# Middle two column groups of an output projection by seven block products instead of eight, and matmuls on zeros at the start

## The chip, the core and the metric

One NeuronCore of a Trainium2 chip runs the whole layer. The metric is device time in microseconds from launch to end, as the median of three runs. TensorE is called PE here, its weight loads PEld, VectorE is DVE, ScalarE is ACT, GpSimd is POOL and SyncE is SP. PE, DVE, ACT and POOL each work through their own queue strictly in the order in which the program was laid down, and an instruction starts when the semaphores that it names have been raised. SP only starts transfers.

## The reference

The layer takes 512 tokens of 2048 channels (and 16 learned tokens ahead of them as further keys), normalises them, multiplies by one wide input projection, runs two attention mixers of 8 heads each, gates both with SiLU, and joins the heads to a matrix of 512 x 2048. What follows is the part that the change is about:

```python
y = jnp.einsum('blc,cd->bld', jnp.concatenate([ya, yb], axis=-1), w_out[layer])
h = h + rmsnorm(y, post_norm_g[layer])
```

The output projection is thus a product of 512 x 2048 by 2048 x 2048, and after it each token's 2048 results are scaled by one number that needs the squares of all of them.

## The kernel before

Everything is float32 in and out. For TensorE each operand is split in two parts of a reduced format, a high part (made by ACT, which rounds) and a low part (made by DVE, the remainder), and each product is three matmuls: high by high, low by high, high by low. The function `wload` (line 142) does it for weights: SP loads 128 x 1024 weights into `st`, ACT writes `wh` (line 150), DVE writes `wl` (line 151). There are three buffers of each, so that the split of a chunk waits until PE has finished with the chunk three before it.

A work list `todo` holds the weight chunks of the whole layer in order of use, and `fetch` hands them out and starts loads two chunks ahead. While PE works through the input projection, tasks (`Lanes`) are put between its matmuls for the attention of the heads; PE's order is the order in which the Python code calls it, while the other engines' instructions are placed by a scheduler with priorities. The negative number `AHEAD` sets how urgent the weights' splits are.

The output projection (`dense_out`, line 723) makes the 2048 output columns in four groups of 512. A group needs 8 chunks of weights, each of which holds 2 of the 16 blocks of 128 rows; for each block and each of the 4 token blocks there are three matmuls of 128 x 128 by 128 x 512, so that a chunk feeds 24 matmuls and a group 192. The stationary operand is the joined heads, `oh` and `ol`, split once and held for all groups: the heads of mixer B and half of mixer A go through a DRAM scratch `oscr` first, the last four heads come straight from SBUF. Group 0 is mixed with the end of the attention. When a group is done, `collect` (line 767) sums squares on ACT and multiplies by the gain `gpB` on DVE, for each of 4 tiles `y` of 128 tokens. In the last group `finish` (line 773) is called for one token block after the other; it makes the scale on POOL, and adds the input `xr` on DVE, except for the last 512 columns, where ACT and POOL do it; SP stores the pieces.

At the start, the first 8 chunks of x and of weights are loaded together (line 207): for each of 16 blocks of x, ACT and DVE make `xh` and `xl`, and 12 matmuls follow.

Of the kernel before, what the change touches and what calls it, by code (L numbers as in the profile page):

```python
# [17 lines left out]
P = 128  # L18
# [90 lines left out]
def kernel(ctx: ExitStack, tc: tile.TileContext, xT, xn, xm, w_s, w_t, w_q, w_o,  # L109
# [19 lines left out]
    oscr = [dr.tile([2, P, SEQ], F32, name=f"oscr{i}", tag=f"oscr{i}") for i in range(6)]  # L129

    def ctile(shape, name, dt=F32, src=None):
        t = cst.tile(shape, dt, name=name, tag=name)
        if src is not None:
            load(t, src)
        return t
# [6 lines left out]
    def wload(src, n=1024, dma=nc.sync.dma_start, parts=1):  # L142
        st = wp.tile([P, 1024], F32, name="st", tag="st")
        wh = wp.tile([P, 1024], F32R, name="wh", tag="wh")
        wl = wp.tile([P, 1024], F32R, name="wl", tag="wl")
        for i in range(parts):
            c = slice(i * n // parts, (i + 1) * n // parts)
            dma(out=st[:, c], in_=src if parts == 1 else src[:, c])
            with tc.high_priority(AHEAD):
                nc.scalar.activation(wh[:, c], st[:, c], AF.Copy)  # L150
                nc.vector.tensor_tensor(out=wl[:, c], in0=st[:, c], in1=wh[:, c].bitcast(F32),  # L151
                                        op=ALU.subtract)
        return wh, wl

# [3 lines left out]
    nc.scalar.activation(warm, epst, AF.Identity)  # L158
    gcol = ctile([P, KT], "gcol")
# [22 lines left out]
    def fetch(ahead=2):  # L182
        while todo and len(chunks) <= ahead:
            chunks.append(wload(todo.pop(0)))
# [81 lines left out]
    cosT = ctile([P, TT, P], "cosT", src=cos_d)  # L266
    sinT = ctile([P, TT, P], "sinT", src=sin_d)
    gqB = ctile([P, P], "gqB", src=gq)
    gkB = ctile([P, P], "gkB", src=gk)
# [235 lines left out]
    def attention_A(h, qn, q_task, k, k_task, v, v_task):  # L505
# [43 lines left out]
        over[NH + h] = last  # L549
        if h < 4:  # L550
            over[NH + h] = lanes.spawn(spill_A(h), 0.0, last)
# [112 lines left out]
    for grp in range(4):  # L664
        todo += [w_o[grp, :, k0:k0 + 2, :] for k0 in range(0, KT, 2)]
# [90 lines left out]
    yp = ctx.enter_context(tc.tile_pool(name="yp", bufs=1))  # L756
    pd2 = ctx.enter_context(tc.tile_pool(name="pd2", bufs=4, space=PSUM))
# [3 lines left out]
    xr = [yp.tile([P, DM], F32, name=f"xr{t}", tag=f"xr{t}") for t in range(TT)]  # L761
    ssy = [yp.tile([P, 4], F32, name=f"ssy{t}", tag=f"ssy{t}") for t in range(TT)]
    for t in range(TT):
        nc.sync.dma_start(out=xr[t], in_=xn[t * P:(t + 1) * P, :])
    sspart = [yp.tile([P, 1], F32, name=f"ssp{t}", tag=f"ssp{t}") for t in range(TT)]

    def collect(g, t, ps):
        gs = slice(g * 512, (g + 1) * 512)
        jk = yp.tile([P, 512], F32, name="jko", tag="jko", bufs=2)
        nc.scalar.activation(jk, ps, AF.Square, accum_out=ssy[t][:, g:g + 1])  # L770
        nc.vector.tensor_tensor(out=y[t][:, gs], in0=ps, in1=gpB[:, gs], op=ALU.mult)

    def finish(t, ps):
# [6 lines left out]
        cuts = [0, 256, 896, 1536, 2048] if last else [0, 1024, 2048]  # L780
        for i, (c0, c1) in enumerate(zip(cuts, cuts[1:])):
            cs = slice(c0, c1)
            if last and i == 3:
                nc.scalar.activation(y[t][:, cs], y[t][:, cs], AF.Copy, scale=r)
                nc.gpsimd.tensor_tensor(out=y[t][:, cs], in0=y[t][:, cs], in1=xr[t][:, cs],
                                        op=ALU.add)
            else:
                nc.vector.scalar_tensor_tensor(out=y[t][:, cs], in0=y[t][:, cs], scalar=r,
                                               in1=xr[t][:, cs], op0=ALU.mult, op1=ALU.add)
            load(out[t * P:(t + 1) * P, cs], y[t][:, cs])  # L790

    for g in range(3):
        pss = first if g == 0 else dense_out(g, pd2 if g % 2 else pd)
        for t in range(TT):
# [65 lines left out]
```

## Time and profile before

| | us |
|---|---|
| median of three runs | 958.59 (957.73 to 961.38) |
| the profiled execution | 958.46 |
| its span, first to last instruction | 956.5 |
| PE busy | 934.7 |
| DVE busy | 525.5 |
| ACT busy | 457.9 |
| POOL busy | 127.7 |
| moved by DMA | 99.31 MB |

The span is 2.0 us shorter than the execution's own time; what lies around it is taken to be the same for both kernels. A row of a timeline gives start, duration, engine, line, operation, the tile written and the tiles read, and a count where equal ones are merged; in brackets stands how long the engine was idle before and who released it. A row of the grouped view gives the busy time and the mean of one in nanoseconds, and then the idle time ahead of them. Matmuls are pipelined: the time that one takes of PE is the distance between two starts, not its duration.

### The profile page before, as it was taken

What the parts mean: (1) busy time and instruction counts of PE and PEld (TensorE: products, weight loads), DVE (VectorE), ACT (ScalarE), POOL (GpSimd) and SP (SyncE); (2) the same over time, 40 slices, a digit from 0 to 9 for tenths busy, and PEclk for the clock granted to TensorE, in tenths of its full rate; (3) what the DMA queues carried; (4) which work ended last, traced back from release to release, by engine and by line L of the source; (5) the groups of instructions that cost most, each with busy time, mean ns of one, the idle gap of its engine ahead of it and who ended that gap; (6) DMA issues with size and microseconds to landing.
All of it is one profiled execution on the core that took longest, in us unless ns stands there. A gap on an engine that the chain in (4) does not pass through costs nothing.

```text
span 956.5 us, 13979 instructions
## 1 busy us (share of the span) xinstructions
PE 934.7 (98%) x5530; PEld 818.2 (86%) x5530; DVE 525.5 (55%) x900; ACT 457.9 (48%) x812; POOL 127.7 (13%) x211
## 2 busy tenths in 40 slices
PE   7999999999999999999999999998999999999996
PEld 6889898989989898998998888886888888888884
DVE  6276675747575574756654274447554663232325
ACT  6665555547464553746552253354555742221221
POOL 0001010101001010100201041225212120000002
PEclk9999999999999999999999999998999999999999
DMA  9752222322223122222223223111222344623314
GB/s 318 252 180 77 85 90 68 97 77 94 82 73 104 66 99 77 86 82 68 91 75 94 94 66 110 57 66 56 77 77 67 114 128 158 238 88 98 101 45 175
DMA packets 31426, 99.31 MB, mean 104 GB/s; under 512 B 3681, under 2 KB 5601, under 8 KB 30721
## 3 DMA queue, kind: packets, MB, share of 16 engines
q1 hardware_dynamic: 31216, 98.42, 31.1%
q8 instruction: 43, 0.70, 0.3%
q14 instruction: 23, 0.18, 0.1%
q10 hardware_dynamic: 144, 0.01, 0.0%
HBM read 91.07 MB, written 7.34 MB: 103 GB/s over the span
## 4 chain that ended last, share of the span: by engine, by line
PE 89%; DVE 4%; ACT 2%; DMA 2%; POOL 2%; issue 1%; SPq 0%; DVEq 0%; POOLq 0%; ACTq 0%
PE pd L63 55%; PE po L63 19%; PE sc L63 6%; PE pv L63 5%; PE tr L66 5%; DMA xns<-in_xn_dram 2%; DVE qn L567 1%; DVE wl L151 1%; POOL ssh L228 1%; ACT qn L639 0%; ACT jk L564 0%; PE ss L63 0%; POOL qn L581 0%; ACT p L537 0%; DMA gcol<-in_gpre_dram 0%
## 5 line engine op out<-in xcount | busy, mean ns | idle before, releaser
L63 PE MATMUL pd<-xh,wh 128*128 128x264 f32 (+1 forms) x992 | 334.8, 337 | 4.9 <-ACT wh L150 4.9
L63 PE MATMUL pd<-xh,wl 128*128 128x264 f32 (+1 forms) x992 | 326.4, 329 | 0.3 <-DVE wl L151 0.3
L63 PE MATMUL pd<-xl,wh 128*128 128x264 f32 (+1 forms) x992 | 326.1, 329 | 0.0
L150 ACT ACTIVATE wh<-st 128x1024 fp32r<-128x1024 f32 (+2 forms) x139 | 144.4, 1039 | 278.0 <-PE po L63 95.8
L151 DVE TENSOR_TENSOR wl<-st,wh 128x1024 fp32r<-128x1024 f32 (+2 forms) x139 | 167.2, 1203 | 176.0 <-ACT wh L150 174.7
L63 PEld LDWEIGHTS pd<-xh,wh 128*128 128x128 f32 x992 | 188.4, 190 | 17.6 <-ACT wh L150 4.9
L63 PEld LDWEIGHTS pd<-xh,wl 128*128 128x128 f32 x992 | 187.7, 189 | 18.0 <-DVE wl L151 0.7
L63 PEld LDWEIGHTS pd<-xl,wh 128*128 128x128 f32 x992 | 188.6, 190 | 11.6
L63 PE MATMUL po<-wh,ol 128*128 128x512 f32 x256 | 101.0, 395 | 0.9 <-DVE ol L296 0.9
L63 PE MATMUL po<-wl,oh 128*128 128x512 f32 x256 | 101.9, 398 | 0.0
L63 PE MATMUL po<-wh,oh 128*128 128x512 f32 x256 | 101.7, 397 | 0.0
L450 ACT ACTIVATE p<-p,mx 128x528 f32<-128x528 f32 x64 | 46.5, 728 | 34.2 <-POOL mx L447 34.0
L63 PEld LDWEIGHTS po<-wh,ol 128*128 128x128 f32 x256 | 48.1, 188 | 12.2 <-DVE ol L296 1.2
L440 DVE CUSTOM_DVE_ANT_0 p<-sc,dist 128x528 f32<-128x528 f32 x64 | 44.9, 701 | 24.0 <-PE sc L63 23.5
L63 PEld LDWEIGHTS po<-wl,oh 128*128 128x128 f32 x256 | 48.1, 188 | 11.2
L63 PEld LDWEIGHTS po<-wh,oh 128*128 128x128 f32 x256 | 48.1, 188 | 10.2
L63 PE MATMUL pd<-wh,xh 128*128 128x512 f32 x128 | 52.2, 408 | 0.8 <-DVE vf L287 0.8
L293 ACT ACTIVATE ph<-tr 128x512 fp32r<-128x512 f32 x64 | 37.6, 591 | 31.2 <-PE tr L66 30.9
L296 DVE TENSOR_TENSOR pl<-tr,ph 128x512 fp32r<-128x512 f32 x64 | 43.4, 688 | 16.1 <-ACT ph L293 14.9
L66 PE MATMUL tr<-ident,p 128*128 128x128 f32 (+1 forms) x320 | 50.8, 273 | 0.8 <-DVE pl L296 0.8
L63 PE MATMUL pd<-wh,xl 128*128 128x512 f32 x128 | 50.6, 395 | 0.0
L63 PE MATMUL pd<-wl,xh 128*128 128x512 f32 x128 | 50.5, 395 | 0.0
(161 smaller groups left out, 1292.1 us busy)
## 6 DMA issues: line engine op xcount, KB each, us to landing
st<-in_w_t_dram SPq DMA_DIRECT2D x82, 512.0 KB, 3.6
st<-in_w_o_dram SPq DMA_DIRECT2D x32, 512.0 KB, 3.6
st<-in_w_q_dram SPq DMA_DIRECT2D x16, 512.0 KB, 3.6
xs<-in_xT_dram SPq DMA_DIRECT2D x16, 264.0 KB, 5.1
xns<-in_xn_dram SPq DMA_DIRECT2D x8, 512.0 KB, 6.3
xr<-in_xn_dram SPq DMA_DIRECT2D x4, 1024.0 KB, 10.2
os<-oscr SPq DMA_DIRECT2D x6, 512.0 KB, 3.6
out_dram<-y SPq DMA_DIRECT2D x6, 512.0 KB, 2.7
```

Of the source, the lines that this page charges most:

```text
L63: self._add(self.nc.tensor.matmul(out, lhsT, rhs, start=start, stop=stop), us)
L66: self._add(self.nc.tensor.transpose(out, in_, ident), 0.109)
L150: nc.scalar.activation(wh[:, c], st[:, c], AF.Copy)
L151: nc.vector.tensor_tensor(out=wl[:, c], in0=st[:, c], in1=wh[:, c].bitcast(F32), op=ALU.subtract)
L228: nc.gpsimd.tensor_tensor(out=dst, in0=dst, in1=mhalf[:rows, :dst.shape[1]], op=ALU.pow)
L293: nc.scalar.activation(dst, src, AF.Copy)
L296: nc.vector.tensor_tensor(out=dst, in0=src, in1=h.bitcast(F32), op=ALU.subtract)
L440: nc.vector.tensor_tensor_reduce(out=two(p), in0=sc[:, :, :HALF], in1=two(dist[:, w0:w0 + NT]), scale=1.0, scalar=-3.0e38, op0=ALU.add, op ...
L450: nc.scalar.activation(p2[m], p2[m], AF.Exp, scale=0.125, bias=mx[:, m:m + 1], accum_out=sm[:, m:m + 1])
L567: nc.vector.scalar_tensor_tensor(out=raw[:, i, :], in0=raw[:, i, :], scalar=ss[:rows, i:i + 1], in1=g[:rows], op0=ALU.mult, op1=ALU.mult)
```

## The change

**The seven products.** Groups 0 and 3 stay as they are. Groups 1 and 2 are seen as a product of 2 x 2 blocks: two halves of the tokens, two halves of the 2048 summed channels (first the heads of mixer B, then those of mixer A), two column groups. Plainly these are eight block products. In their place stand seven, in the way of Strassen and Winograd: four of them multiply sums of blocks. Each block product takes 4 chunks of weights and 2 token blocks, 12 matmuls to a chunk, 48 in all.

- Weights: tiles `ch0` to `ch3` hold a running sum of blocks. POOL's queue loads block (1, 0) and then adds (1, 1) by an accumulating transfer; after each split (`wsplit`, ACT and DVE as before) the next block is loaded into `st` and added on DVE (`summed`).
- Heads: the halves of `oscr` (now all 16 heads are written there) are loaded into a ring of five tiles `ts`, on POOL's queue for the first two sums (`first_sums`) and on SP's for the others. DVE forms the sums, ACT and DVE split them (`operand`).
- Results: products leave PSUM by an ACT copy or by DVE sums into the tiles `y`; the squares are taken by ACT from `y`, and the gain is multiplied on POOL (`block_done`).
- The input `xr` is loaded on POOL's queue, in 16 pieces, into tiles that the operands leave; `finish` adds in pieces of 512 columns.
- The priority of the weight splits is changed (`rank`) once the attention is over.

**The zeros.** A tile `heat` of 128 x 256 zeros is written by DVE, and 16 matmuls multiply it by itself ahead of all others.

```diff
+    heat = ctile([P, 256], "heat", F32R, pool=ap)
+    nc.vector.memset(heat.bitcast(F32), 0.0)
+    hot = pd.tile([P, 512], F32, name="hot", tag="pd")
+    for i in range(16):
+        mm(hot[:, :256], heat[:, :P], heat, start=True, stop=True)
...
+    def summed(add=None, fresh=None):
+
+        def step(i):
+            ws = wsplit(chain[i])
+            if fresh:
+                nc.sync.dma_start(out=chain[i], in_=block(*fresh, i))
+            if add:
+                st = wp.tile([P, 1024], F32, name="st", tag="st")
+                nc.sync.dma_start(out=st, in_=block(*add, i))
+                with tc.high_priority(rank[0]):
+                    nc.vector.tensor_tensor(out=chain[i], in0=chain[i], in1=st, op=ALU.add)
+            return ws
+        return [lambda i=i: step(i) for i in range(4)]
...
+    todo += whole(0) + plain(0, 0) + plain(0, 1) + summed((0, 0)) + summed((0, 1))
+    todo += summed((1, 0), fresh=(0, 0)) + summed() + plain(1, 1) + whole(3)
...
+    rank[0] = 40
...
+    def heads_of(i, half, dma):
+
+        t = yp.tile([P, 2, NP], F32, name="ts", tag="ts", bufs=5)
+        dma.dma_start(out=t, in_=oscr[i].rearrange("i p q -> p i q")[:, :, half])
+        return t
+
+    def operand(tag, i, src):
+
+        h, l = [yp.tile([P, 2, NP], F32R, name=f"{tag}{x}{i}", tag=f"{tag}{x}{i}") for x in "hl"]
+        hi(h, src)
+        lo(l, src, h)
+        return h, l
+
+    for i in range(4):
+        chain[i] = yp.tile([P, 1024], F32, name=f"ch{i}", tag=f"ch{i}")
+        nc.gpsimd.dma_start(out=chain[i], in_=block(1, 0, i))
+    t1, t2, t3, t4 = [], [], [], []
+
+    def first_sums(i):
+        b0, b1, a1 = [heads_of(j, half, nc.gpsimd)
+                      for j, half in ((i, lo_), (i, hi_), (4 + i, hi_))]
+        nc.gpsimd.dma_start(out=chain[i], in_=block(1, 1, i), accum_op=ALU.add)
+        TTv(out=b0, in0=b1, in1=b0, op=SUB)
+        t1.append(operand("u", i, b0))
+        TTv(out=a1, in0=a1, in1=b0, op=SUB)
+        t2.append(operand("v", i, a1))
+
+    def third_sum(i):
+        b1, a1 = heads_of(i, hi_, nc.sync), heads_of(4 + i, hi_, nc.sync)
+        TTv(out=a1, in0=a1, in1=b1, op=SUB)
+        t3.append(operand("u", i, a1))
+
+    def fourth_sum(i):
+        a0 = heads_of(4 + i, lo_, nc.sync)
+        TTv(out=a0, in0=t2[i][0].bitcast(F32), in1=a0, op=SUB)
+        TTv(out=a0, in0=a0, in1=t2[i][1].bitcast(F32), op=ALU.add)
+        t4.append(operand("v", i, a0))
...
+    def product(ops, pool):
+
+        pss = [pool.tile([P, 512], F32, name="po", tag="pd") for _ in range(2)]
+        for i in range(4):
+            wh, wl = fetch()
+            for u in range(2):
+                for j in range(2):
+                    bh, bl = ops(i, j, u)
+                    c = slice(j * 512, (j + 1) * 512)
+                    mm(pss[u], bh, wh[:, c], start=(i + j == 0), stop=False)
+                    mm(pss[u], bl, wh[:, c], start=False, stop=False)
+                    mm(pss[u], bh, wl[:, c], start=False, stop=(i + j == 4))
+        return pss
...
+    def block_done(r, x, u):
+        g = 1 + r
+        square(2 * x + u, g, C(r, x, u))
+        TTp(out=C(r, x, u), in0=C(r, x, u), in1=gpB[:, g * 512:(g + 1) * 512], op=ALU.mult)
...
+    for i in range(4):
+        first_sums(i)
+    for u, ps in enumerate(product(of_y(0, 0), pd2)):
+        nc.scalar.activation(C(1, 0, u), ps, AF.Copy)
+    for u, ps in enumerate(product(of_y(1, 0), pd2)):
+        TTv(out=C(0, 0, u), in0=ps, in1=C(1, 0, u), op=ALU.add)
+        block_done(0, 0, u)
+    for u, ps in enumerate(product(of_t(t1), pd)):
+        nc.scalar.activation(C(1, 1, u), ps, AF.Copy)
+    for i in range(4):
+        third_sum(i)
+    for u, ps in enumerate(product(of_t(t2), pd)):
+        TTv(out=C(1, 0, u), in0=ps, in1=C(1, 0, u), op=SUB)
+        TTv(out=C(0, 1, u), in0=C(1, 0, u), in1=C(1, 1, u), op=ALU.add)
+    for i in range(4):
+        fourth_sum(i)
+    for u, ps in enumerate(product(of_y(1, 1), pd2)):
+        TTv(out=C(0, 1, u), in0=ps, in1=C(0, 1, u), op=SUB)
+        block_done(0, 1, u)
+    for u, ps in enumerate(product(of_t(t3), pd2)):
+        TTv(out=C(1, 0, u), in0=C(1, 0, u), in1=ps, op=SUB)
+        TTv(out=C(1, 1, u), in0=C(1, 0, u), in1=C(1, 1, u), op=ALU.add)
+        block_done(1, 1, u)
+    for u, ps in enumerate(product(of_t(t4), pd)):
+        TTv(out=C(1, 0, u), in0=C(1, 0, u), in1=ps, op=SUB)
+        block_done(1, 0, u)
...
```

In what follows the seven products are called P1 to P7 in this order, and their 28 chunks of weights c0 to c27.

**DVE, groups 1 and 2.** In the kernel before, DVE's whole work for a group of 45 us is eight splits and four products by the gain (the rows are those of group 1):

```order
L771 TENSOR_TENSOR y_8191<-po,gpB 128x512
L771 TENSOR_TENSOR y_8192<-po,gpB 128x512
L771 TENSOR_TENSOR y_8193<-po,gpB 128x512
L151 TENSOR_TENSOR wl<-st,wh 128x1024
L771 TENSOR_TENSOR y_8194<-po,gpB 128x512
L151 TENSOR_TENSOR wl<-st,wh 128x1024 x7
```

In the changed kernel this is DVE's queue from the split of c20 (the first row, for the start of P6) to that of c21 (the last); `ts` and `vl` belong to the operands of P7, `ch_8220` to chunk c23:

```order
L155 TENSOR_TENSOR wl<-ch_8214,wh 128x1024
L701 TENSOR_TENSOR ch_8220<-ch_8220,st 128x1024
L309 TENSOR_TENSOR vl_8681<-ts,vh_8680 128x512
L842 TENSOR_TENSOR ts<-ts,vl_8279 128x512
L841 TENSOR_TENSOR ts<-vh_8295,ts 128x512
L841 TENSOR_TENSOR ts<-vh_8312,ts 128x512
L842 TENSOR_TENSOR ts<-ts,vl_8296 128x512
L309 TENSOR_TENSOR vl_8689<-ts,vh_8688 128x512
L842 TENSOR_TENSOR ts<-ts,vl_8313 128x512
L309 TENSOR_TENSOR vl_8697<-ts,vh_8696 128x512
L155 TENSOR_TENSOR wl<-ch_8216,wh 128x1024
```

Between two splits that followed each other directly there now stand one sum of weights and eight operations on operands of the next product. Over the stretch from the first operand's sum (line 829) to the split of c21, DVE's queue holds 30 operations of 128 x 1024 (18 splits and 12 sums of weights) and 41 of 128 x 512.

**POOL's queue.** Before, POOL had nothing to do from the end of the attention to the first `ry`. Now, after the last row of the attention (`pm`), it starts these transfers:

```order
L413 TENSOR_SCALAR pm<-pm 32x256 x3
L822 DMA ch_8214<-in_w_o_dram 128x1024
L822 DMA ch_8216<-in_w_o_dram 128x1024
L822 DMA ch_8218<-in_w_o_dram 128x1024
L822 DMA ch_8220<-in_w_o_dram 128x1024
L810 DMA ts<-oscr_78 128x2x256 x2
L810 DMA ts<-oscr_82 128x2x256
L828 DMA ch_8214<-in_w_o_dram 128x1024
L810 DMA ts<-oscr_79 128x2x256 x2
L810 DMA ts<-oscr_83 128x2x256
L828 DMA ch_8216<-in_w_o_dram 128x1024
L828 DMA ch_8218<-in_w_o_dram 128x1024
```

The same queue goes on with the rest of the first operands, and then with its first two products by the gain:

```order
L810 DMA ts<-oscr_80 128x2x256 x2
L810 DMA ts<-oscr_84 128x2x256
L810 DMA ts<-oscr_81 128x2x256
L828 DMA ch_8220<-in_w_o_dram 128x1024
L810 DMA ts<-oscr_81 128x2x256
L810 DMA ts<-oscr_85 128x2x256
L889 TENSOR_TENSOR y_8224<-y_8224,gpB 128x512
L889 TENSOR_TENSOR y_8225<-y_8225,gpB 128x512
```

The rows of line 828 are the accumulating transfers. The loads of the third and fourth operand pair (`oscr_80`, `oscr_81`) stand behind them, and each `ts` also waits until DVE has done with the tile of the ring that it takes.

116 lines of the change are left out of this document (71 added, 45 removed).

## The prediction

> **What bounds the kernel now.** I read the busy times first, then what PE waits for, then the timeline of the output projection.
>
> ```profile
> PE 934.7 (98%) x5530; PEld 818.2 (86%) x5530; DVE 525.5 (55%) x900; ACT 457.9 (48%) x812; POOL 127.7 (13%) x211
> PE pd L63 <- ACT wh L150: 4.9, 1, 4.9
> PE sc L63 <- ACT p L537: 3.0, 1, 3.0
> PE tr L63 <- DVE rm L247: 1.3, 1, 1.3
> ```
>
> The second to fourth rows are what PE waited for in all, how often and the longest. Ahead of the first matmul it waits 4.9 us, and nowhere else over 3 us: PE sets the time, and what is to be seen is whether it keeps doing so where the change puts work on others. The timeline of ACT shows the groups' length, and windows over groups 1 and 2 show what the others do there:
>
> ```profile
> 811.27 0.60 ACT L770 ACTIVATE jko<-po 128x512 f32<-128x512 f32 x1 [2.68 <-PE po L63]
> ...
> 856.02 0.60 ACT L770 ACTIVATE jko<-po 128x512 f32<-128x512 f32 x1 [2.68 <-PE po L63]
> ...
> 900.82 0.60 ACT L770 ACTIVATE jko<-po 128x512 f32<-128x512 f32 x1 [2.68 <-PE po L63]
> core 0: us, PE busy (x) PEld busy (x) DVE busy (x) ACT busy (x) POOL busy (x), PEclk, DMA share, GB/s
> 813.00:858.00 45.00, 45.00 (x195) 36.19 (x194) 12.68 (x13) 11.21 (x18) 0.00 (x0) 1.00 0.49 174
> 858.00:903.00 45.00, 45.00 (x195) 36.19 (x194) 12.62 (x14) 11.21 (x19) 0.00 (x0) 1.00 0.31 94
> ```
>
> The first squares of two groups start 44.8 us apart (900.82 - 856.02). That is 192 matmuls at 233 ns, without a gap, while DVE works 12.7 us of 45 and POOL none. DVE has over 30 us of room in each group, which the change uses up.
>
> **The change part by part.** (1) *Removed matmuls.* 56 blocks of 12 for 64: 336 matmuls for 384, so 48 x 0.233 = 11.2 us less, all on the path. A product lasts 11.2 us now, and a chunk is used up in 2.8 us where it lasted 5.6.
>
> (2) *The zeros.*
>
> ```profile
> 4.89 0.59 PE L63 MATMUL pd<-xh,wh 128*128 128x264 f32 x1 [4.89 <-ACT wh L150]
> ...
> 6.97 1.62 ACT L167 ACTIVATE xh<-xs,gcol 128x528 fp32r<-128x528 f32 x2
> 7.23 0.63 PE L63 MATMUL pd<-xl,wh 128*128 128x512 f32 x1
> ...
> 7.65 0.63 PE L63 MATMUL pd<-xh,wl 128*128 128x512 f32 x1
> 7.74 1.65 DVE L168 SCALAR_TENSOR_TENSOR xl<-xs,gcol,xh 128x528 fp32r<-128x528 f32 x2 [0.32 <-ACT xh L167]
> ...
> 11.02 0.40 PE L63 MATMUL pd<-xl,wh 128*128 128x512 f32 x1
> 11.25 0.39 PE L63 MATMUL pd<-xh,wl 128*128 128x512 f32 x1
> ...
> 12.18 0.28 PE L63 MATMUL pd<-xh,wh 128*128 128x264 f32 x1
> ```
>
> Until about 10.7 us a matmul of 512 columns takes 0.42 us (7.65 - 7.23), from then on 0.23 (11.25 - 11.02), though the clock column shows 1.0 there. It turns 5.8 us after PE's start. Sixteen matmuls of 256 columns at the slow pace last 16 x 0.21 = 3.4 us and lie in the 4.9 us in which PE waits anyway. If the turn comes 5.8 us after these, it is at about 7 us. The fast pace is worth less than half of the slow stretch, since the second block of x is late next: its `xh` is there at 7.8 us (half of the ACT row), its `xl` at 8.6, and 11 fast matmuls behind that (2.0 us) end at 10.6, where before the second block ended at 12.18. So 1.5 us is gained, at most 1.6. At least it is nothing: at 49 us PE waits 1.3 us for `rm`, and if that chain, which begins with loads of x, did not move along, the gain would be waited away there. It starts from a weight split that PE releases, so I take 1.5.
>
> (3) *DVE's queue.* This is where I see the price. The spacing of operations that follow each other is the cost:
>
> ```profile
> 754.77 3.09 DVE L296 TENSOR_TENSOR ol<-os,oh 128x512 fp32r<-128x512 f32 x5
> ...
> 903.96 1.22 DVE L151 TENSOR_TENSOR wl<-st,wh 128x1024 fp32r<-128x1024 f32 x1
> 905.10 0.68 DVE L771 TENSOR_TENSOR y<-po,gpB 128x512 f32<-128x512 f32 x1
> ...
> 818.68 1.06 ACT L150 ACTIVATE wh<-st 128x1024 fp32r<-128x1024 f32 x1 [3.79 <-PE po L63]
> 819.77 1.23 DVE L151 TENSOR_TENSOR wl<-st,wh 128x1024 fp32r<-128x1024 f32 x1 [3.60 <-ACT wh L150]
> ```
>
> A split of 1024 takes DVE 1.14 us (905.10 - 903.96), an operation of 512 takes 0.60 ((3.09 - 0.69) / 4), and a split starts 1.09 us after ACT's part. The sums of weights have no row; they are 128 x 1024 float32 from SBUF like the split, so 1.14.
>
> Count from the start of P1. The split of c3 needs the buffer that c0 leaves at 2.8 us and is done at 2.8 + 1.09 + 1.14 = 5.0. Behind it in DVE's queue stand, up to the split of c21, 30 operations of 1024 and 41 of 512: 34.2 + 24.6 = 58.8 us, so that it ends at 63.8 even if DVE never waits. PE needs it with the third matmul of c21: 21 x 2.8 + 0.5 = 59.3. PE is thus held up by 4.5 us, nearly all of it between c20 and c21: up to c19 the same sum is 2.8 us or more ahead, c20 is due at 56.5 and ready at 56.8, and then come nine others, 1.14 + 8 x 0.60 = 5.9 us, ahead of the split of c21. ACT's splits wait for none of this: 28 of 1.06 and about as many small ones fill less than 50 of 78 us.
>
> (4) *DVE's waits* lengthen this one for one. At least: the split of c15 can't start before c12 is used up (13 x 2.8 = 36.4, + 1.09 + 1.14 = 38.6), and DVE comes to it at 36.9 at the end of its work: 1.7 us idle. More comes from the loads of `ts`, which DVE takes in order:
>
> ```profile
> st<-in_w_o_dram SPq DMA_DIRECT2D x32, 512.0 KB, 3.6
> oscr<-gB SPq DMA_DIRECT2D x8, 256.0 KB, 2.0
> 10.00:20.00 10.00, 10.00 (x56) 8.80 (x55) 8.98 (x12) 7.25 (x11) 0.00 (x0) 1.00 1.04 398
> ```
>
> The last rows' figures are the size, the time to land, and 398 GB/s as the most that a window shows. The fourth pair's first sum is DVE's turn at 17.4 us. Its load waits for a tile of the ring, which DVE's first sum leaves at 5.6 us for the load two pairs earlier; between these POOL's queue starts six loads of 0.26 MB and three accumulating ones of 0.52 MB, and SP eight chunks: 7.3 MB. If each were there in time, the idle time stays at 1.7; if all went ahead of it at 398 GB/s, it would land at 5.6 + 18.4 + 2.0 = 26, 8.6 us late. Since SP's later chunks are not ahead of it, I take 5, between these.
>
> The accumulating transfer has no row. Its nearest one is the plain load (3.6 us), its lower bound; above I allow four times the transfer (rival D). The Trainium skill (DMA: Bandwidth & Descriptors, Anatomy of one DMA — SWDGE (gpsimd) path) prices a transfer from POOL's queue at 2.0 us and its bytes at 436 GB/s, an estimate of 2.6 us for a `ts`; no row here shows one, and the sum would stay as it is.
>
> (5) *POOL beside DVE.* Two products by the gain fall into the stretch.
>
> ```profile
> L788 DVE SCALAR_TENSOR_TENSOR y<-y,ry,xr 128x1024 f32<-128x1024 f32 x6 | 7.4, 1280 | 1.0 <-POOL ry L778 1.0
> L788 DVE SCALAR_TENSOR_TENSOR y<-y,ry,xr 128x640 f32<-128x640 f32 x2 | 2.7, 1380 | 0.0
> L581 POOL TENSOR_TENSOR kn<-kn,cosT 128x512 f32<-128x512 f32 x2 | 2.6, 1295 | 2.3 <-DVE t L579 2.3
> L785 POOL TENSOR_TENSOR y<-y,xr 128x512 f32<-128x512 f32 x1 | 1.6, 1602 | 0.8 <-ACT y L784 0.8
> ```
>
> The two DVE operations of 640 columns ran while POOL ran line 785, and took 1.38 us each, more than 1024 columns elsewhere; at 1.28 x 640 / 1024 they should take 0.80. One POOL product thus cost DVE 1.2 us. Two cost 2.4 at most, nothing where DVE reads PSUM just then; I take 1.2. The Trainium skill (SBUF — State Buffer, Who interferes with whom) has DVE and GpSimd exclude each other for a whole instruction where DVE reads two operands from SBUF and GpSimd reads too. By that the two would cost 2 x 1.3 = 2.6, and the sum would be 1.4 us more; the row of 1.38 us agrees with it.
>
> (6) *The rest.* The end has one DVE operation more on its path (four for three at the same columns): + 0.1. The loads of `xr` move from SP to POOL's queue, behind P6, with over 40 us until `finish` reads them, and no row makes me cost them.
>
> *Sum:* -11.2 - 1.5 + 4.5 + 5 + 1.2 + 0.1 = -1.9 us on the profiled 958.46: 956.6, and 956.7 against the median, which lies 0.13 us above that execution. Ends of the unknowns: 958.6 - 11.2 - 1.6 + 4.5 + 1.7 = 952.0, and 958.6 - 11.2 + 4.5 + 8.6 + 2.4 + 0.1 = 963.0. What a measurement of this kernel can tell from no change is about 0.5%, 4.8 us: no change is 953.8 to 963.4.
>
> **The rivals.** *A, the forecast:* DVE becomes the bound of P3 to P6 and gives most of the 11.2 us back. Chance 0.54.
>
> *B: the loads are in time and POOL is not in DVE's way:* 952.0. For it speaks that DMA is half idle there (0.49 and 0.31); against it that one ring of five tiles ties each load to DVE. 0.16.
>
> *C: DVE does not bind at all,* the whole gain stays: 958.6 - 11.2 - 1.5 = 945.9. It would need DVE to do 1024 columns in 1.0 us and 512 in 0.5, and no row shows that. 0.05.
>
> *D: slower.* The accumulating transfers are slow, and hold up the loads behind them in POOL's queue. At a quarter of 398 GB/s each takes 5.3 us where a plain one takes 1.3; the three ahead of the fourth pair add 11.8 us to DVE's 5 us of waiting: 956.7 + 11.8 = 968.5. It makes the kernel slower by over 0.5% once DVE waits over 11.7 us in all (5 + 963.4 - 956.7). Nothing in the profile speaks against it, as no such transfer is in it. 0.17.
>
> *E: the zeros do nothing* (the pace turns at the same time, or the gain is lost at 49 us), all else as in A: 958.2. 0.08.
>
> **How the numbers follow.** Forecast: 956.7 us, by itself 953.8 to 961. The range is 951.0 to 966.0: B's 952.0 and the upper end of 963.0 lie in it, and a part of D; C and the rest of D are outside. Faster by over 0.5%: B, C and a little of A's lower side, 0.25. Within it: most of A and E, 0.55. Slower: D and a little of A's upper side, 0.20.
>
> **What would show it.** Right: DVE over 90% busy from P3 to P6, PE waiting for `wl` early in P6, above all at c21, 6 us or more in all over the products; 48 matmuls less; the 512 columns at 0.23 us from about 7 us on and the second block done at 10.6. D would show as DVE waiting for `ts`, and ACT for `ch`, around P1 to P3. Wrong: PE without waits from P1 to P7, or PE waits before c8 that are longer than those at c21, would leave step 3 without its place; a spacing of DVE's operations other than 1.14 and 0.60 would leave it without its price.

## The result, and the profile after

| | before | after |
|---|---|---|
| median, us | 957.73 (956.64 to 961.38, 5 runs) | 966.93 (964.95 to 967.23, 5 runs) |
| the profiled execution | 958.46 | 966.93 |
| its span | 956.5 | 965.2 |
| PE busy | 934.7 | 930.0 |
| DVE busy | 525.5 | 581.5 |
| moved by DMA, MB | 99.31 | 117.16 |

After takes 1.0086 times as long as before (95% interval 1.0064 to 1.0108): slower by 0.9%, where no change was forecast. Line numbers from here on are those of the changed kernel; c0 to c27 are the weight chunks of the products P1 to P7, four each.

First comes what PE waited for in the output projection (total, times, longest), then the rows of PE's timeline at four of the six places.

```profile
PE po L63 <- DVE wl L155: 16.5, 6, 6.9
...
836.59 0.79 PE L63 MATMUL po<-wl,oh 128*128 128x512 f32 x1 [6.85 <-DVE wl L155]
...
875.56 0.50 PE L63 MATMUL po<-wl,oh 128*128 128x512 f32 x1 [2.20 <-DVE wl L155]
...
881.64 0.79 PE L63 MATMUL po<-wl,uh 128*128 128x512 f32 x1 [3.02 <-DVE wl L155]
882.23 0.63 PE L63 MATMUL po<-wh,uh 128*128 128x512 f32 x1
882.65 0.63 PE L63 MATMUL po<-wh,ul 128*128 128x512 f32 x1
...
890.62 0.50 PE L63 MATMUL po<-wl,uh 128*128 128x512 f32 x1 [3.50 <-DVE wl L155]
```

Where before had no wait at all, PE waits 16.5 us for splits by DVE: once long, before c7, and then at c19, c20 and c21. Behind the long gaps a matmul of 512 columns takes 0.42 us (882.65 - 882.23) and not 0.23. The windows show it as the granted clock (the third number from the end; behind it DMA share and GB/s).

```profile
core 0: us, PE busy (x) PEld busy (x) DVE busy (x) ACT busy (x) POOL busy (x), PEclk, DMA share, GB/s
820.00:824.00 4.00, 4.00 (x19) 3.22 (x18) 3.98 (x6) 3.04 (x5) 2.42 (x5) 1.00 0.98 213
824.00:828.00 4.00, 4.00 (x19) 3.23 (x18) 1.10 (x2) 0.16 (x2) 2.27 (x3) 1.00 1.04 261
828.00:832.00 4.00, 1.70 (x7) 0.73 (x5) 0.00 (x0) 0.95 (x1) 0.00 (x0) 1.00 1.03 353
832.00:836.00 4.00, 0.00 (x0) 0.00 (x0) 1.99 (x3) 1.20 (x3) 0.72 (x1) 0.65 1.07 287
836.00:840.00 4.00, 3.41 (x8) 2.73 (x9) 3.50 (x6) 1.98 (x4) 0.00 (x0) 0.50 0.92 285
...
884.00:888.00 4.00, 3.12 (x8) 1.91 (x6) 2.19 (x4) 2.07 (x3) 1.13 (x2) 0.52 0.43 156
...
892.00:896.00 4.00, 4.00 (x14) 3.17 (x13) 2.86 (x5) 1.93 (x4) 1.37 (x2) 0.67 0.03 7
```

From 824 to 836 DVE works 3.1 of 12 us while the DMA engines are full; they are full or nearly so from 820 to 840, and move only 213 to 353 GB/s. DVE's own timeline, with one row of POOL's at the end, names its waits:

```profile
811.91 1.89 DVE L858 TENSOR_TENSOR y<-po,gpB 128x512 f32<-128x512 f32 x3 [5.97 <-DMA gpB<-in_gpost_dram]
...
815.44 1.21 DVE L155 TENSOR_TENSOR wl<-st,wh 128x1024 fp32r<-128x1024 f32 x1
...
833.98 0.69 DVE L829 TENSOR_TENSOR ts<-ts 128x512 f32<-128x512 f32 x1 [8.88 <-DMA ts<-oscr]
...
873.14 1.23 DVE L701 TENSOR_TENSOR ch<-ch,st 128x1024 f32<-128x1024 f32 x1 [0.85 <-DMA ch<-in_w_o_dram]
...
887.54 0.69 DVE L309 TENSOR_TENSOR vl<-ts,vh 128x512 fp32r<-128x512 f32 x1 [1.81 <-ACT vh L306]
...
889.35 1.22 DVE L155 TENSOR_TENSOR wl<-ch,wh 128x1024 fp32r<-128x1024 f32 x1
...
817.56 0.71 POOL L810 DMA_DIRECT2D ts<-oscr x1 [13.37 <-DVE ts L829]
```

DVE waits 6.0 us for the gain vector behind group 0, then 8.9 us for the third pair of heads. The split of c3 starts at 815.44, that of c21 at 889.35. POOL's queue stood still for 13.4 us, since the ring's next tile came free with DVE's first sum.

At the start of the kernel the zeros do, in this execution, what was expected of them: from 7.2 us on 512 columns take 0.24 us.

```profile
1.21 3.78 PE L63 MATMUL hot<-heat 128*128 128x256 f32 x16 [1.21 <-DVE heat L167]
...
7.22 0.40 PE L63 MATMUL pd<-xl,wh 128*128 128x512 f32 x1
7.46 0.39 PE L63 MATMUL pd<-xh,wl 128*128 128x512 f32 x1
...
46.47 1.40 PE L63 MATMUL tr<-dg,ones 128*128 128x512 f32 x4
```

The same four matmuls of the last row in before:

```profile
49.24 1.60 PE L63 MATMUL tr<-dg,ones 128*128 128x512 f32 x4 [1.27 <-DVE rm L247]
```

They start 2.8 us earlier, and the wait for `rm` is gone.

**The balance.** Group 0's first square starts at 807.30 for 811.27 (-4.0). The last one of group 3 follows at 956.03 for 947.78, so the projection takes 12.2 us more. That is -11.2 for 48 matmuls, 16.5 of waits, and about 7 that are left. Most of these are the half clock: by the distance of the matmuls' starts it cost 1.9 us behind the gap at c7, 2.8 behind c20 and 1.5 behind c21.

### The profile page after: what moved, and what is told of

The parts are those of the page before. It is cut to its first block, busy times and chain, and to the rows that moved or that the text cites. A ratio compares the mean times of both kernels' runs of the same rounds, so it can differ in the third digit from the quotient of the medians.

```text
span 965.2 us, 14195 instructions
## 1 busy us (share of the span) xinstructions
PE 930.0 (96%) x5498; PEld 812.2 (84%) x5498; DVE 581.5 (60%) x974; ACT 481.7 (50%) x844; POOL 162.9 (17%) x255
## 2 busy tenths in 40 slices
DMA packets 39811, 117.16 MB, mean 121 GB/s; under 512 B 4640, under 2 KB 9632, under 8 KB 39616
## 4 chain that ended last, share of the span: by engine, by line
PE 80%; DVE 7%; DMA 5%; POOL 3%; ACT 3%; issue 2%; SPq 0%; DVEq 0%; POOLq 0%; ACTq 0%
PE pd L63 54%; PE po L63 11%; PE sc L63 6%; PE pv L63 4%; PE tr L66 4%; DMA ts<-oscr 2%; DVE wl L155 2%; DVE qn L578 1%; POOL qn L592 1%; DMA ch<-in_w_o_dram 1%; POOL ssh L241 1%; DMA os<-oscr 1%; DVE ch L701 1%; DMA xs<-in_xT_dram 1%; ACT qn L650 0%
## 5 line engine op out<-in xcount | busy, mean ns | idle before, releaser
L154 ACT ACTIVATE wh<-st 128x1024 fp32r<-128x1024 f32 (+2 forms) x135 | 140.2, 1039 | 226.7 <-PE pd L63 91.0
L155 DVE TENSOR_TENSOR wl<-st,wh 128x1024 fp32r<-128x1024 f32 (+2 forms) x135 | 162.6, 1205 | 117.4 <-ACT wh L154 116.1
L63 PEld LDWEIGHTS pd<-xl,wh 128*128 128x128 f32 x992 | 187.5, 189 | 11.7 <-DVE xl L180 0.4
L63 PE MATMUL po<-wl,oh 128*128 128x512 f32 x176 | 70.5, 401 | 9.0 <-DVE wl L155 9.0
L63 PE MATMUL po<-wh,oh 128*128 128x512 f32 x176 | 71.2, 405 | 0.0
L63 PE MATMUL po<-wh,ol 128*128 128x512 f32 x176 | 70.3, 399 | 0.9 <-DVE ol L309 0.9
L66 PEld LDWEIGHTS tr<-ident,p 128*128 128x128 f32 (+1 forms) x320 | 37.2, 131 | 14.0 <-DVE gA L558 2.4
L63 PEld LDWEIGHTS po<-wl,oh 128*128 128x128 f32 x176 | 33.4, 190 | 18.2 <-DVE wl L155 10.3
L460 POOL TENSOR_SCALAR mx<-mx 128x2 f32<-128x2 f32 x32 | 12.1, 377 | 196.0 <-DVE mx L453 196.0
```

What stands on the lines that cost most here:

```text
L63: self._add(self.nc.tensor.matmul(out, lhsT, rhs, start=start, stop=stop), us)
L66: self._add(self.nc.tensor.transpose(out, in_, ident), 0.109)
L460: nc.gpsimd.tensor_scalar(out=mx, in0=mx, scalar1=-0.125, scalar2=1.0, op0=ALU.mult, op1=ALU.mult)
```

## The experiments

Three explanations of DVE's long wait stood against each other: the accumulating transfers are slow and hold up POOL's queue (theory 1), the DMA engines have too many bytes there in whatever form (rival 1), the ring of five tiles (rival 2). Beside them stood the order of DVE's queue, the clock, and the zeros. Ratios are to runs of before on the same chip.

**Plain loads for the accumulating ones.**

```diff
-        nc.gpsimd.dma_start(out=chain[i], in_=block(1, 1, i), accum_op=ALU.add)
+        nc.gpsimd.dma_start(out=chain[i], in_=block(1, 1, i))
```

> The four accumulating loads of the chains become plain loads of the same bytes into the same tiles, with every instruction of all queues in the same place; left out is block (1,0) of the weights in the first sum, so two products are computed from other weights, for the same work. Theory 1 (the accumulating transfers are slow and hold up the loads queued behind them): the 8.88 us for which VectorE waited at the third pair falls below 4 us, TensorE's wait at c7 (6.85 us) below 2 us, the half-clock stretch behind it (836 to 840) goes, and c19 to c21, 8.7 us in all, shrink too since VectorE starts its queue earlier: 945 to 958, say 953. Rival 1 (the 16 DMA engines have too much to move there, in whatever form): same bytes, same waits, 964 to 968. Rival 2 (the ring of five ts tiles is issued too late): the order and the waits of the queue are the same, 964 to 968.

Measured: 964.19 us, ratio 1.0043 (1.0024 to 1.0063). DVE's long wait:

```profile
DVE ts L829 <- DMA ts<-oscr: 6.3, 1, 6.3
```

and POOL's DMA queue from 780 to 860 (packets, MB, share of 16 engines), first in after, then here:

```profile
q0 software_dynamic: 2112, 7.34, 32.4%
```

```profile
q0 software_dynamic: 2112, 7.34, 25.9%
```

The same packets took 6.5% of 80 us less, 5.2 us of all sixteen engines for four transfers: in these two traces an accumulating transfer of 512 KB costs 1.3 us of them more than a plain one. The engines are still full, but move more:

```profile
828.00:832.00 4.00, 2.77 (x12) 1.87 (x10) 0.00 (x0) 0.94 (x1) 0.00 (x0) 1.00 1.02 386
```

The three loads of the third pair were under way for 12.2 to 13.1 us in after, and for 9.8 to 11.4 here. DVE's wait shrinks by 2.6 us only, and the end by 2.7 (by the two ratios 4.1). Theory 1 is a third of the wait at most.

**The first sums' loads on SP's queue.**

```diff
-        b0, b1, a1 = [heads_of(j, half, nc.gpsimd)
+        b0, b1, a1 = [heads_of(j, half, nc.sync)
```

> The twelve loads of ts for the first sums go through SP's queue instead of POOL's; the accumulating ones stay on POOL's. Theory 1: they land in about 5.5 us as the other ts of SP's queue did, VectorE's wait at the third pair is below 3 us, TensorE's at c7 below 2 us, in all 948 to 958, unless SP, held by the ring of five, brings the weights' st late, which would show as ScalarE waiting for st in the first two products. Rival 1 (bytes): the waits stay at 5 to 9 us, 963 to 968. Rival 2 (ring): the loads still wait for a free tile, about 6 us late at the third pair, 962 to 968.

Measured: 964.37 us, ratio 1.0052 (1.0033 to 1.0072). DVE's waits, and one window:

```profile
DVE y L858 <- DMA gpB<-in_gpost_dram: 7.1, 1, 7.1
DVE ts L829 <- DMA ts<-oscr: 6.5, 2, 5.1
...
816.00:820.00 4.00, 0.21 (x1) 0.00 (x0) 0.00 (x0) 0.00 (x0) 0.00 (x0) 1.00 1.04 256
```

The loads wait no less behind another queue: the first five were under way for 16.6 to 17.0 us. They only tell at another place (PE stands for 6.4 us at c2, until 822.6), with the DMA engines full at 256 GB/s. So POOL's queue isn't what binds. The Trainium skill (DMA: Bandwidth & Descriptors, Issuing engines are not separate DMA queues) has the transfers that any engine issues end up on the same sixteen engines. This run agrees.

**The zeros alone, and the change without them.** The diff is the `heat` block of the change, put into before, or taken from after.

> The kernel before with the sixteen products on zeros ahead of x, and nothing else of the change. By the trace of after the zeros are worth 2.9 us from 47.5 us on (faster clock from 7.0 us, and a wait for rm of 1.27 us gone); the further 1.1 us ahead of the output projection come from the other edits: 957.7 - 2.9 = 954.8 (954 to 955.5), ratio 0.997. Rival: all 4.0 us come from the zeros, 953.7. Rival: what the zeros win is lost again before the end, as a wait on a load takes it up, 957.7.

Measured: 955.60 us, ratio 0.9957 (0.9941 to 0.9974), the first square of group 0 at 808.54.

> After without the products on zeros. If the zeros are worth 2.9 us and the other 1.1 us ahead of the output projection come from elsewhere: 966.9 + 2.9 = 969.8, with the first jko (group 0's end) at 810.2. If all 4.0 are the zeros': 970.9, with the first jko at 811.3 as before. If the zeros' gain is taken up later: 966.9.

Measured: 968.83 us in one execution, 1.9 us above after, with the first square at 810.65. The zeros are worth about 2.8 us by the traces (811.27 - 808.54 = 2.7; spans 956.5 - 953.7), and 2.5 to 5.7 us by the interval of the ratio. In the profiled executions of kernels with zeros shown here, that square starts between 806.2 and 809.7 us, so the further 1.2 us in after lie within the scatter.

**Rank 120 for 40.**

```diff
-    rank[0] = 40
+    rank[0] = 120
```

> Splits and sums of the weights get rank 120 for 40 in the order that the planner writes; the work is the same. In VectorE's queue the third and fourth sums of P6 and P7 then stand behind the splits of c18 to c23. By the prediction's sum (1.14 and 0.60 us, no waits) the split of c21 is ready at 54.3 us from the start of P1 for 63.8, 5.0 ahead of its need at 59.3, and all other chunks are 4 to 8 us ahead. After has VectorE 17.3 us later than the sum (2.2 at c3, 12.5 of waits, 2.6 of longer operations), so that TensorE stays 12 us late for 21.8. Theory (order of VectorE's queue plus its waits): 966.9 - 9.8 = 957, TensorE's waits for wl 8 to 12 us, the most of it at c7. Rival (VectorE's total of work binds, in whatever order): c22 to c27 are late in place of c20 and c21, 964 to 968.

Measured: 958.32 us, ratio 1.0001 (0.9988 to 1.0015), 1.3 us above the expected 957. What PE waited for, and the longest of it:

```profile
PE po L63 <- DVE wl L155: 8.9, 3, 6.5
...
838.12 0.80 PE L63 MATMUL po<-wl,oh 128*128 128x512 f32 x1 [6.47 <-DVE wl L155]
```

The waits at c20 and c21 are gone; the one at c7 stays, and 1.9 us at c19. Step 3 is right: the hold-up there was the order of DVE's queue and not its total of work.

**The gain vector first.**

```diff
+    gpB = [yp.tile([P, 512], F32, name=f"gpB{g}", tag=f"gpB{g}") for g in range(4)]
+    nc.gpsimd.dma_start(out=gpB[0], in_=gpost[:, 0:512])
...
-    nc.sync.dma_start(out=gpB, in_=gpost)
```

> The gain vector is loaded in four quarters, the first on POOL's queue ahead of the chains, the others on SP's where the whole was. VectorE no longer waits 6.0 us for it behind group 0. Theory (a late start of VectorE leaves the ring's tiles late, so that the third pair's loads are issued late): the first sum runs at about 2.2 us after the start of P1 in place of 7.2, the ring's first tile is free 4 to 5 us earlier, the wait at the third pair falls from 8.9 to about 5, TensorE's wait at c7 from 6.9 to 0 to 2, and the end comes 3 to 6 us earlier: 961 to 964. Rival (the bytes of that stretch bind, and what starts earlier only waits longer): third pair at the same time as before, 12.5 us of waits become 18, 965 to 967.

Measured: 961.72 us, ratio 1.0041 (1.0025 to 1.0056), as the theory has it. DVE's waits for `ts` fall to 3.3 and 1.9 us, PE's at c7 to 1.1, with 3.0 more at c8; early in P6 PE still waits 5.6. The step by which the theory gets there is not what the trace shows. The third pair's loads start no earlier after the start of P1 than in after (822.5 for 810.8, and 820.0 for 809.2). They are under way for 4.4 to 6.3 us and not for 12.2 to 13.1, behind one accumulating transfer in POOL's queue where two had just started in after.

**Both together, and POOL's queue in another order.**

```diff
+    early = [three(i) for i in range(2)]
...
+        if i == 0:
+            for k in range(4):
+                nc.gpsimd.dma_start(out=chain[k], in_=block(1, 1, k), accum_op=ALU.add)
+        b0, b1, a1 = early[i] if i < 2 else three(i)
```

> Rank 120, the gain vector in quarters, a ring of six, and POOL's queue in another order: six ts of the first two pairs, then the chains, then the four accumulating loads, then the six ts of the last two pairs. Theory (order plus loads, no lack of bytes): VectorE's waits between c3 and c21 fall from 12.5 to 3 to 6 us, less than the 4 to 8 us that each chunk is ahead; TensorE waits 0 to 3 us in the products and its clock stays full: 966.9 - 21.8 - 1.7 + 0 to 3 = 943.5 to 947. Rival (the DMA engines are full from P1 to P3, so VectorE's loads come as late as now in whatever order): 953 to 957, as with rank 120 alone.

Measured: 960.76 us, ratio 1.0025 (1.0015 to 1.0035): 14 us above the theory, and above its rival too. Windows, and two rows of PE's timeline:

```profile
820.00:824.00 4.00, 4.00 (x19) 3.23 (x18) 0.81 (x2) 1.54 (x2) 2.31 (x4) 1.00 1.04 272
824.00:828.00 4.00, 4.00 (x19) 3.05 (x17) 1.42 (x2) 1.55 (x2) 0.72 (x1) 1.00 1.06 275
828.00:832.00 4.00, 3.51 (x13) 2.10 (x12) 1.42 (x2) 2.01 (x2) 0.00 (x0) 1.00 1.03 298
832.00:836.00 4.00, 3.07 (x12) 2.17 (x12) 0.69 (x2) 0.00 (x0) 0.00 (x0) 1.00 1.04 383
...
890.31 0.50 PE L63 MATMUL po<-wh,vh 128*128 128x512 f32 x1 [2.78 <-ACT vh L306]
892.05 0.79 PE L63 MATMUL po<-wh,vl 128*128 128x512 f32 x1 [1.24 <-DVE vl L309]
```

The early start is lost again: in these 16 us DVE is idle for 11.7 (4.34 busy), in after for 8.9. From 808 to 836 it worked 14.7 us here and 15.1 in after. The first sum of the third pair starts 24.7 us after the start of P1, in after 24.8. So with the engines full, another order of loads gains nothing for it. And with rank 120 the fourth sums, late with everything else, came too late for P7.

**Matmuls on zeros in PE's gaps.**

```diff
+    FILL, used = {20: 11, 21: 20}, [0]
...
+                    for _ in range(FILL.get(used[0] - 1, 0) if u + j == 0 else 0):
+                        mm(pss[u], zero, wh[:, c], start=False, stop=False)
                     mm(pss[u], bh, wl[:, c], start=False, stop=(i + j == 4))
```

> After with 11 and 20 products on zeros, added into the running sum, ahead of the third matmul of c20 and of c21, where TensorE waits 3.0 and 3.5 us; VectorE's and ScalarE's order is the same. They last 2.6 and 4.7 us at 0.233 and lie in the waits (with c20 at full clock the wait at c21 would be 3.5 + 2.5). Theory (TensorE's end is set by the split of c21, and behind its wait the clock costs 0.37 + 0.5 + 0.5 + 0.34 = 1.7 us): the granted clock stays at 1.0 from 881 to 896 and the end comes 1.7 us earlier, 965.2. Rival (all of the slow stretches, about 7 us, lie on the path): 960. Rival (idle gaps aren't what lowers the clock): 966.9, still .50 there.

Measured: 963.71 us in two executions (962.58 and 964.85), ratio 1.0059 (1.0039 to 1.0079), 3.2 us below after where 1.7 was expected; the two intervals overlap. Two windows, and the split of c21:

```profile
884.00:888.00 4.00, 4.00 (x19) 3.33 (x18) 4.00 (x7) 1.91 (x4) 0.41 (x1) 1.00 0.56 196
...
892.00:896.00 4.00, 4.00 (x20) 3.30 (x19) 2.83 (x2) 2.09 (x4) 3.93 (x4) 1.00 0.78 242
...
886.49 1.22 DVE L155 TENSOR_TENSOR wl<-ch,wh 128x1024 fp32r<-128x1024 f32 x1
```

The clock stays at 1.0, so PE's gaps are what lowered it. The split of c21 itself starts 2.9 us earlier (886.49 for 889.35). Of these, 1.0 us is there already at the split of c20 (879.37 for 880.36), which the fills don't reach; the 1.8 us for which DVE waited for ACT are gone. The span is 4.4 us shorter in these two executions, so about 3.4 of it comes from the fills. A slow PE leaves the weight buffers late; that the late buffers held ACT up, and ACT DVE, is my reading and was not run by itself.

**Small loads for the accumulating ones.**

```diff
-        nc.gpsimd.dma_start(out=chain[i], in_=block(1, 1, i), accum_op=ALU.add)
+        nc.gpsimd.dma_start(out=chain[i][:, 0:8], in_=block(1, 1, i)[:, 0, 0:8])
```

> The four accumulating loads of 512 KB become plain ones of 4 KB (8 columns of each row), so that 2.1 MB less are moved in P1 to P3; left out is nearly all of block (1,1) of the weights in the first sum, for the same work on TensorE. Up to the third pair VectorE's order differs by one split. Theory (the sixteen DMA engines are full there, whatever the form of a transfer): 2.1 MB at the 280 GB/s that the full windows 820 to 836 of after show are 7.5 us; the wait at the third pair falls from 8.9 (6.3 with plain loads of full size) to 0 to 2, TensorE's at c7 to 0 to 2, and since the queue's order still holds c20 and c21 up, the end is at 957 to 960. Rival (the ring of five lets the third pair's loads be issued too late): its first load still waits 13 us for a tile in POOL's queue, VectorE waits 5 us or more, 963 to 965.

Measured: 958.20 us, ratio 1.0000 (0.9989 to 1.0011).

```profile
DVE ts L829 <- DMA ts<-oscr: 2.5, 1, 2.5
```

Without the 2.1 MB the wait is 2.5 us, and the three loads of the third pair are under way for 5.0 to 5.9 us. Taken away in this order, of 8.9 the accumulating form made 2.6, the bytes 3.8, and 2.5 are left. POOL's queue still stood 10.4 us for the ring, so rival 2 makes 2.5 us at most here; rival 1 is the largest part. The profiled execution (954.66 us) is the fastest of eight, and three of the small loads stand ahead of POOL's wait for the ring, where one accumulating load stood in after.

**The plain group 3 ahead of the products.** If the late start is all, 45 us of room should win everything.

```diff
-    todo += whole(0) + plain(0, 0) + ...
+    todo += whole(0) + whole(3) + plain(0, 0) + ...
```

> After with the plain last column group put ahead of the seven products, which now come last; the rows are finished two behind P6 and two behind P7, whose last three chunks go row tile by row tile. So the chains, the first sums' loads and the first sums have 45 us more, in which VectorE worked 12.7 us. Theory (bytes and VectorE's queue bind only because P1 to P3 follow at once): TensorE waits under 1 us in the products, clock 1.0 throughout: 957.7 - 2.9 (zeros) - 11.2 (48 matmuls) + 1.5 (0 to 4 for two rows to be finished behind the last product) = 945 (943.5 to 949). Rival (VectorE's total of work in P3 to P7, not the late start, binds): waits for wl of 5 us or more in P5 to P7, 950 to 957.

> The same with rank 120 for 40. Theory: with the loads in time the order of VectorE's queue no longer matters, since by the sum of 1.14 and 0.60 us each split is in time in both; within 1 us of the former, 945. Rival (order matters still, or the fourth sums come too late for P7): 2 us or more apart from it.

Measured: 958.17 us, ratio 1.0001 (0.9992 to 1.0010), and 958.44 with rank 120; 13 us above the expectation. The windows of the second and two rows of its DVE show where that lies:

```profile
932.00:938.00 6.00, 3.80 (x17) 2.82 (x15) 3.26 (x4) 1.34 (x3) 5.00 (x6) 1.00 0.38 158
938.00:944.00 6.00, 0.00 (x0) 0.00 (x0) 4.37 (x5) 1.44 (x3) 3.03 (x4) 0.74 0.47 192
...
941.14 0.67 DVE L973 TENSOR_TENSOR y<-y,po 128x512 f32<-128x512 f32 x1
...
947.16 0.67 DVE L973 TENSOR_TENSOR y<-y,po 128x512 f32<-128x512 f32 x1
```

PE is done before 938, and the rest of the 957.6 us is the end: the second row's difference stood behind the first row's scaled sums. The products had become fast, and my new end gave the gain back.

**A shorter end.**

```diff
         block_done(1, 0, u)
-        finish(u, xr[u])
+    for t in (0, 1):
+        finish(t, xr[t])
```

> g3_rank120 with another end: both differences of P7 ahead of the scaling of rows 0 and 1 in VectorE's queue (there the second one stood behind three scaled sums that waited for the first row's root: 941.1 and 947.2, with TensorE done at about 937), the products by the gain of the last block on VectorE for POOL, and rows 0 and 1 of x loaded through SP's queue into the ring of ts. Theory (g3_first had the products' time as expected, and lost it behind TensorE's end): TensorE ends at 936 to 937, both differences by 938, root 2 us later, seven scaled sums of 1.03 in all by 946 to 947, output 2 to 3 us later: 949 to 951, ratio 0.992. Rival (the products themselves are the loss): TensorE's end is later by what is taken off behind it, 956 to 958.

Measured: 954.49 us, ratio 0.9956 (0.9942 to 0.9970), 3.5 us above the expectation: the two differences start at 939.0, and seven scaled sums still follow them.

**Half of group 3 ahead.** The end stays as in after.

```diff
-    todo += whole(0) + plain(0, 0) + ... + plain(1, 1) + whole(3)
+    todo += whole(0) + whole(3)[:4] + plain(0, 0) + ... + plain(1, 1) + whole(3)[4:]
...
+    half = dense_out(3, pd2, k1=8)
```

> After with the plain last column group cut in two: its first four chunks (22.4 us) run between group 0 and P1, its other four behind P7 with the end as it was; the products use the other four banks throughout. Rank 40 as in after. Theory (loads and VectorE are late by 12.5 + 2.2 us at P1 to P3 and by the order's 4.5 us at c21, and by nothing else): 22.4 us of room cover them, TensorE waits 0 to 3 us in the products, clock 1.0: 957.9 - 2.9 - 11.2 + 0 to 3 = 944 to 947, ratio 0.987. Rival (the products have a loss of their own, a full DMA or VectorE's total of work): waits for wl or vh of 6 us or more in P4 to P7, 950 to 958.

> The same with rank 120. Theory: with 22.4 us of room both orders have each split in time by the sum of 1.14 and 0.60 us (0.1 us of waits with 40, none with 120), so within 1.5 us of the former: 944 to 947. Rival (order still decides at c20 and c21): 3 us or more below the former. Rival (at rank 120 the fourth sums come too late for P7): 2 us or more above it.

Measured: 953.04 us, ratio 0.9951 (0.9936 to 0.9966), and 951.88 us, 0.9934 (0.9920 to 0.9949). The order hardly matters now, as expected, but both are 5 to 6 us above the upper end of the expectation, mainly for one stall (4.9 us in the first kernel, which also waits 2.2 us at 899.9). Here it is in the second kernel, with two rows of DVE's timeline:

```profile
843.72 0.79 PE L63 MATMUL po<-wl,oh 128*128 128x512 f32 x1 [4.59 <-DVE wl L155]
...
841.84 0.69 DVE L836 TENSOR_TENSOR ts<-ts 128x512 f32<-128x512 f32 x1 [2.02 <-DMA ts<-oscr]
842.45 1.22 DVE L155 TENSOR_TENSOR wl<-st,wh 128x1024 fp32r<-128x1024 f32 x1
```

The scheduler uses the room to put third sums ahead of the split, and their loads aren't there yet. The clock is 0.59 in the 8 us from 840.

**Half of group 3, and the gain vector first.** The diff is that of the gain vector above, on top of the last kernel.

> half_ahead_120 with the gain vector in quarters, the first ahead of the chains on POOL's queue. Theory (the one stall left, 4.6 us at 843 and 8 us x 0.41 of clock behind it, follows from VectorE's 5.6 us of waiting for the gain vector and the ring's tiles that come free late): VectorE starts its first sums 4 to 5 us earlier, the third sums' loads start 4 to 5 us earlier, the stall is 0 to 1.5 us and the clock stays 1.0: 951.9 - 4.6 - 3.3 + 0 to 2 = 944 to 946. Rival (the DMA engines are full from 808 to 840, and the third sums' loads land no earlier): stall of 3 us or more, 949 to 952.

Measured: 946.19 us, ratio 0.9866 (0.9850 to 0.9883). The one wait for a split that is left, and DVE's first row behind group 0:

```profile
844.08 0.50 PE L63 MATMUL po<-wl,oh 128*128 128x512 f32 x1 [1.75 <-DVE wl L155]
...
809.37 2.17 DVE L858 TENSOR_TENSOR y<-po,gpB 128x512 f32<-128x512 f32 x3 [2.09 <-ACT jko L853]
...
840.00:848.00 8.00, 6.25 (x22) 4.60 (x22) 5.48 (x6) 2.14 (x3) 0.00 (x0) 0.83 0.85 271
```

It is 1.3% faster than before, and by the two ratios (0.9866 and 0.9957) about 9 us faster than the zeros alone. The clock did not stay at 1.0, though: from 845.4 to 848.4 the matmuls start 0.43 us apart, behind a gap of only 1.75 us. In the profiled execution (948.23 us, the slowest of four) 128.8 us pass from the first square of group 0 to the last of group 3 (808.65 to 937.47), where before takes 136.5. That is 7.7 of the 11.2 us of the removed matmuls. The other 3.5 are about the stall: 1.75 and 0.3 us of waits, and 1.6 of half clock. So the seven products show no loss beside it. They need room ahead of them, for loads and for DVE.

## Why the prediction was wrong

**Step 1** (-11.2): right, 48 matmuls at 0.233; the last kernel keeps 7.7 of it in its profiled execution.

**Step 2** (zeros, -1.5, at most 1.6): the mechanism and the second block's end (10.85 us, 10.6 forecast) were right, the size was not. That the pace turned 5.9 us after PE's first matmul, as I took it from before (5.8), was luck: with the same sixteen matmuls it turned 2.9 us after it in the zeros alone (at 4.1 us), and 9.3 us after it with rank 120 (at 10.5). I wrote that the wait for `rm` could take the gain away; in after it went away itself (1.27 us). With the zeros alone 0.99 us of it stays, the matmuls behind it start 1.7 us earlier (47.50 for 49.24), and group 0's first square 2.7 us earlier; where the last 1.0 us comes from is not shown. Rival E is refuted.

**Step 3** (DVE's queue, 4.5): right in work, price and order. From the split of c3 to that of c21 the trace has 30 operations of 1024 and 41 of 512 and the spacings 1.14 and 0.60. Its start was taken too early: the split of c3 ends 7.4 us after P1's start (809.2) for 5.0, since DVE stood 6 us waiting for the gain vector, a wait that the sum put at nothing. DVE was busy for 48.3 of the 51.6 us from 839.0 to 890.6 (94%), as the sign of being right asked for.

**Step 4** (DVE's waits, 5 between 1.7 and 8.6) is the term that failed. Between c3 and c21 they are 12.5 us: 8.88 for the third pair, 1.0 for two later `ts`, 0.85 for `ch`, 1.81 for `vh`. I divided bytes by 398 GB/s, the best that a window of before showed; the full windows of P1 to P3 moved 213 to 353. I counted from the first sum, too, and not the transfers that start before it, the chains and the gain vector. And I looked for the jam at the fourth pair, where it is at the third: its loads were under way for 12.2 to 13.1 us, and with 2.1 MB less in the way for 5.0 to 5.9.

**Step 5** (POOL beside DVE, 1.2): DVE's operations around POOL's two products took 1.6 us longer (852 to 856), within the range.

**A term that was missing:** behind its gaps PE runs at half clock. Most of that is covered, since the split of c21 sets the time anyway; behind c21 it cost 1.7 us by the estimate made for the fills, 1.5 by the distance of the matmuls' starts. With the gaps at c20 and c21 filled, the end came 3.2 us earlier by the medians; of the 4.4 us between the two profiled executions, about 3.4 come from the fills.

**The sum again**, from P1's start to the split of c21: 7.4 + 58.8 + 12.5 + 2.6 of longer operations and short gaps (1.6 of them beside POOL's products) = 81.3 us, where the prediction had 5.0 + 58.8 + 5 + 1.2 = 70.0. With 1.7 of clock, 0.4 at the end, -1.3 for the zeros and -1.2 of scatter that makes 10.9 us more than forecast; the profiled execution has 10.3 more than the 956.6 of the sum.

**Rival D** came nearest (968.5 us), but for a reason that is only part of the cause: the accumulating form made 2.6 of the 8.9 us, the bytes more, and the queue behind which the loads stood little (with SP's queue the end came 2.6 us earlier). Its point of decision, 11.7 us of DVE's waits, held: they were 12.5. Rivals B and C fell with the waits. My sign of error in step 3, longer waits before c8 than at c21, occurred, and yet the step stood: both held, one after the other, which I hadn't allowed for.

**The granted clock** was 0.50 behind gaps of 3.0 to 6.9 us, and full again 3.3 us after the end of the gap of 6.85 (at 839.9). The Trainium skill (TensorE: Matmul & The Clock Gate, What's actually happening) has half rate after an idle window of about 3.4 us and full rate after one that is busy; the trace of after agrees within half a microsecond, for the gap at c20 (3.0) with the shorter one of 2.2 at c19 ahead of it. Other runs do not: half clock followed gaps of 1.75 us (the last kernel), 1.86 (the small loads) and 1.94 (rank 120 alone), while none followed gaps of 2.18 (half of group 3 ahead, rank 40) and 2.89 (both together, POOL's queue in another order). So the length of a gap alone does not decide it; what else does is not shown here.

## What to carry to other kernels

When matmuls are traded for sums and transfers, add up the bytes that must land before the first new operand is used, with those already under way, and divide by a rate that such transfers reach when mixed. A saving that holds only if loads and an in-order engine start early needs a stretch of plain work ahead of it: putting half of an unchanged group there was worth more than any tuning of the queues. And a wait of PE can cost more than its length: behind a gap of 1.75 us the clock was at half for 3 us.

## What the runs showed that I had not expected

- By the two traces, an accumulating transfer of 512 KB took 1.3 us of all sixteen DMA engines more than a plain one, which at 398 GB/s takes 1.3: about twice as much.
- The sixteen engines were full or nearly so (share 0.98 and more) at 213 to 299 GB/s in several windows with accumulating transfers. With plain ones in their place the windows from 824 to 832 moved 370 and 386 GB/s, where after moved 261 and 353. Whether another transfer is slow too stays open.
- Loads in another order, with the same bytes, let DVE do the same work by 836 us (14.7 and 15.1 us of it from 808 on).
- Sixteen matmuls on zeros in time that PE waits for its first load are worth 2.8 us by the traces, and by the ratio 0.9957 more (2.5 to 5.7 us).
